# One fp32 transformer block on one core: the selected-key attention placed right behind the top-k search in program order

## The chip, the core and the metric

The kernel runs on one core of a Trainium2 chip. The core's engines are TensorE (PE, matmuls; PEld is its weight load), VectorE (DVE), ScalarE (ACT), GpSimd (POOL) and SyncE (SP, which here only issues DMAs; ACT issues some too). Each engine runs its own instructions in their order, and waits for the others through semaphores. The metric is the device time of one execution in microseconds (us), lower is better; the times given are the median of several runs.

## What is computed

One transformer block on 512 rows of width 1024, in fp32: a mixer of three attention branches whose outputs are projected up, gated and added, then attention to a memory of 256 rows, then a SwiGLU. Cut to the mixer, which the change touches, and to the part behind it:

```python
p = _split_columns(u @ w_in)
o_a = _stick_breaking(...)                 # first branch
o_b = _dsa_attention(..., q_idx, k_idx, w_idx)   # second branch, on selected keys
o_c = _nsa_attention(...)                  # third branch
g = sigmoid(p['g_merge'].reshape(B, S, 3, D_MODEL))
merged = g[:, :, 0] * (o_a @ w_up[0]) + g[:, :, 1] * (o_b @ w_up[1]) + g[:, :, 2] * (o_c @ w_up[2])
h = x + merged @ w_out
kv = (_rmsnorm(mem, g_kv) @ w_kv)          # memory keys and values: no input from the mixer
```

In the second branch an index score of each row against each earlier row is made, the 128 largest of them are found (`top_k`), and the softmax runs over these keys alone.

## The kernel before

Rows are held in NT = 4 tiles of 128, columns in NK = 8 tiles of 128. An fp32 matmul is made of three passes of a reduced fp32 type, high·high, high·low and low·high (mm3, L91 to L96; the rows of the profile name them L94, L95, L96 in the order in which the scheduler put them; one of them is called a step below). So every weight block is loaded by SP (L80), cast to its high part by ACT (L58) and subtracted to its low part (L66), by DVE for `load_split` (three buffers) and by POOL for `load_fill` (two buffers).

The program is written stage by stage, and a scheduler gives each engine its order when the kernel is built: what stands earlier in the text has priority, and later work is drawn forward where the scheduler's own estimate sees an engine free. On the chip the order is then fixed. Moving a stage in the text therefore changes with what its instructions are interleaved. The stages that matter, in the order of the text before:

- The third branch's attention, per row tile three `rows_attention` or `cmp_attention` calls (L570 to L610) into one accumulator `av` (one PSUM bank). A call makes per head a score (L292, L293) into a bank of `gm` (two banks), DVE adds the mask and reduces it (L578), ACT takes the exponential (L579); the rows are scaled (L588 on DVE for the selected keys, L586 on ACT else), transposed by PE (L565) into `ps` (three banks), copied to SBUF (L60 by DVE for the selected keys, L58 by ACT else) and multiplied with the values (L101, two matmuls of two passes: x4 in the rows).
- Gates of the first branch, `fill_gate(0, f)` for f from 3 on: 24 steps into a bank of `gf` (two banks), then a tanh (L373). Then `merge_up(0, "a")` (merge a below): per f 6 steps `gf<-o_hi..` and a DVE product L388, 48 steps in all.
- Gates of the third branch, `fill_gate(2, f)`, 8 of 24 steps of 512 columns.
- The top-k search: 16 rounds over three tiles of score rows, each round a MAX8 (L615) and a MATCH_REPLACE8 (L616), all on DVE.
- `merge_up(2, "c")` (merge c): 48 steps into `gm`, 8 L388 on DVE, 8 additions on POOL (L404).
- L638 turns the searched score rows into a mask (three DVE instructions on SBUF), and the selected-key attention follows, 16 heads in four row tiles (scores `gm<-kb_hi,qi`, value products `av<-pt,vb`).
- Gates of the second branch for half of the rows, `fill_gate(1, f, S // 2)`: 8 of 24 steps of 256 columns.
- The memory's keys and values (L660 to L683): its rows `h` are loaded on ACT's queue (L664), normed (a square on ACT, L127; ten or so DVE instructions of one column, L115 to L120; a scaling, L129), transposed (L133) and multiplied with weights (48 steps of 512 columns, L94 to L96 on `mg_hi`, `mg_lo`). Then comes the merge of the second branch.

In the order that the chip runs before, merge a goes along with the third branch's last row tile while DVE searches; the third branch's gates and merge c follow, and then the selected-key attention, with the second branch's gates between its instructions on PE.

Of the kernel before, what the change touches and what calls it, by code (L numbers as in the profile page):

```python
# [18 lines left out]
NK = D // P  # L19
# [7 lines left out]
def block_kernel(ctx: ExitStack, tc: tile.TileContext, A, out, dbg=None):  # L27
# [6 lines left out]
    def dump(name, ap):  # L34
        if dbg and name in dbg:
            nc.sync.dma_start(dbg[name], ap)
# [25 lines left out]
    def split(dst_hi, dst_lo, src, hi_eng=None, lo_eng=None, scale=None):  # L62

        if scale is None:
            copy(hi_eng or nc.scalar, dst_hi, src)
            (lo_eng or nc.vector).tensor_sub(dst_lo, src, dst_hi.bitcast(F32))  # L66
        else:
            nc.scalar.activation(dst_hi, src, AF.Copy, scale=scale)
            nc.vector.scalar_tensor_tensor(dst_lo, src, scale, dst_hi.bitcast(F32), op0=ALU.mult, op1=ALU.subtract)

    def ring(pl, bufs, hi_eng=None, lo_eng=None):

        def load(shape, parts, lo_eng=lo_eng):
            n = shape[0] * shape[1]
            raw = pl.tile([P, WT], F32, name="raw", bufs=bufs[0])
            rv = raw[:, :n].rearrange("p (k n) -> p k n", n=shape[1])
            off = 0
            for src in parts:
                w = src.shape[-1]
                nc.sync.dma_start(rv[:, :, off:off + w], src)  # L80
                off += w
            hi = pl.tile([P, WT], F32R, name="whi", bufs=bufs[1])
            lo = pl.tile([P, WT], F32R, name="wlo", bufs=bufs[1])
            split(hi[:, :n], lo[:, :n], raw[:, :n], hi_eng, lo_eng)
            return [t[:, :n].rearrange("p (k n) -> p k n", n=shape[1]) for t in (hi, lo)]
        return load

    load_split = ring(stage, (3, 3))
    load_fill = ring(fill, (2, 2), lo_eng=nc.gpsimd)
# [56 lines left out]
    def cc(c):  # L146
        return slice(c * P, (c + 1) * P)
# [4 lines left out]
    gf_ps = pm.enter_context(tc.tile_pool(name="gf_ps", bufs=2, space=PSUM))  # L152
# [3 lines left out]
    gm_ps = gf_ps  # L156
# [206 lines left out]
    early_g = 3  # L363

    def merge_gate(j, f, g, load, bank, cols=slice(0, S)):

        w = load((NK, P), [col_view(w_in, 2128 + j * D + f * P, P)])
        for k in range(NK):
            mm3(bank, [t[:, k, :] for t in w], [t[:, k, cols] for t in uT], k == 0, k == NK - 1)
        if j == 0 and f < early_g:  # L370
            nc.scalar.copy(g, bank)
        else:
            nc.scalar.activation(g, bank, AF.Tanh, scale=0.5)  # L373

    def fill_gate(j, f, n=S):
        g_t[j, f] = gp_.tile([P, S], F32, name="g", bufs=16)
        gp = gf_ps.tile([P, 512], F32, name="gf")
        merge_gate(j, f, g_t[j, f][:, :n], load_split if j == 1 and f % 2 else load_fill, gp[:, :n], slice(0, n))

    def load_up(j, fh, load):  # L380
        return load((2, 512), [A["w_up"][0, j].rearrange("(k p) n -> p k n", p=P)[:, :, fh * 512:(fh + 1) * 512]])

    def add_up(w, f, name, g, up, cols):

        fc = slice(f % 4 * P, f % 4 * P + P)
        for k in range(2):
            mm3(up, [t[:, k, fc] for t in w], [t[:, k, cols] for t in oT[name]], k == 0, k == 1)
        nc.vector.scalar_tensor_tensor(g, g, 1.0, up, op0=ALU.add, op1=ALU.mult)  # L388

    def merge_up(j, name, load, up_ps, n=S):  # L390
        for f in range(NK):
            if f % 4 == 0:
                w = load_up(j, f // 4, load)
            g, first = g_t[j, f][:, :n], g_t[0, f][:, :n]
            if j == 0 and f < early_g:
                with tc.issue_after(last_exp[0]):
                    nc.scalar.activation(g, g, AF.Tanh, scale=0.5)
            up = up_ps.tile([P, 512], F32, name=up_tag[up_ps is gf_ps])
            add_up(w, f, name, g, up[:, :n], slice(0, n))
            if j == 1:  # L400
                nc.vector.tensor_add(first, first, g)
                split(mg[0][:, f, :n], mg[1][:, f, :n], first, lo_eng=nc.gpsimd)
            elif j == 2:
                nc.gpsimd.tensor_add(first, first, g)  # L404
# [8 lines left out]
    gm_ps = pm.enter_context(tc.tile_pool(name="gm_ps", bufs=2, space=PSUM))  # L413
# [198 lines left out]
    def topk_rounds(i, n):  # L612
        for _ in range(n):
            m8 = mq.tile([P, 8], F32, name="m8", bufs=3)
            nc.vector.max(m8, score[i])  # L615
            nc.vector.match_replace(score[i], m8, score[i], -3e38)  # L616
# [6 lines left out]
        rows_attention(i, qc, kwin, vs["vwin"], causal_bias(i), gates[:, i, 2::3], o_ps, False, True)  # L623
        split(o_c[0][:, :, cc(i)], o_c[1][:, :, cc(i)], o_ps, scale=0.5)
    dump("o_c", o_c[0].bitcast(F32))
    for f in range(early_g, NK):
        fill_gate(0, f)
    merge_up(0, "a", load_fill, gf_ps)
    for f in range(NK):
        fill_gate(2, f)  # L630
    for r in range(16):
        for x in range(1, NT):
            topk_rounds(x, 1)
    merge_up(2, "c", load_split, gm_ps)


    for i in range(1, NT):
# [2 lines left out]
    for i in range(NT):  # L640
        o_ps = av_ps.tile([P, 2, P], F32, name="av")
        rows_attention(i, qb, kb, vs["vb"], score[i] if i else causal_bias(0), None, o_ps, True, True, nc.vector)
        split(o_b[0][:, :, cc(i)], o_b[1][:, :, cc(i)], o_ps, scale=0.5)
    dump("o_b", o_b[0].bitcast(F32))
    for f in range(NK):
        fill_gate(1, f, S // 2)
    mq_st.close()
# [278 lines left out]
```

## Time and profile before

| what | us |
|---|---|
| median of 3 runs (901.30 to 902.61) | 902.41 |
| the profiled execution | 901.59 |
| its span in the trace | 899.8 |
| PE busy within the span | 859.8 (96%) |
| DVE busy | 509.5 (57%) |
| ACT busy | 412.3 (46%) |
| POOL busy | 139.0 (15%) |

All times below are counted from the start of the span. The profiled execution lies 0.82 us below the median and 1.79 us above its own span. The page gives the shares, windows cut the span into stretches, the timeline has single instructions with the idle time ahead of each in square brackets and what ended it. Matmuls are pipelined, so a row's duration is longer than its distance to the next row: what a step costs is that distance.

### The profile page before, as it was taken

Reading aid. Unit: us, or ns where it says so; the run is one execution under the profiler, and the core shown is the slowest. Engines: PE = TensorE matmul, PEld = TensorE weight load, DVE = VectorE, ACT = ScalarE, POOL = GpSimd, SP = SyncE. Lnnn points to the kernel's source line nnn. Section 1 sums busy time; section 2 is a strip of 40 time slices with the busy share of each in tenths; the row PEclk is TensorE's granted clock in tenths of the full one; section 3 lists DMA queues with packets and bytes.
Section 4 is the critical chain, followed back from the end, with each engine's and each line's share of the span. In section 5 each row is a group of like instructions: output and inputs, shape, how many; then the busy total and the mean of one; then the engine's idle time right before and its main releaser. Section 6 shows DMA issues by size and latency. Waiting matters only on the chain.

```text
span 899.8 us, 13079 instructions
## 1 busy us (share of the span) xinstructions
PE 859.8 (96%) x5012; PEld 734.3 (82%) x5012; DVE 509.5 (57%) x1155; ACT 412.3 (46%) x779; POOL 139.0 (15%) x116
## 2 busy tenths in 40 slices
PE   5999999899999999899989999999999999999995
PEld 5987899887768877778878979998888888888884
DVE  4456378799992067676677758544434333322226
ACT  6488545567772234554655546432232233211123
POOL 4021232202224462230232020000000000000002
PEclk9999999999999999999999999999999999999998
DMA  9340114511212332558445514553333333332312
GB/s 322 84 110 24 52 49 121 139 48 34 62 48 71 94 94 71 186 173 241 128 148 187 178 48 131 179 160 93 94 95 101 105 98 94 117 94 93 97 45 93
DMA packets 93710, 99.00 MB, mean 110 GB/s; under 512 B 4656, under 2 KB 81616, under 8 KB 93648
## 3 DMA queue, kind: packets, MB, share of 16 engines
q1 hardware_dynamic: 91568, 92.75, 34.1%
q10 hardware_dynamic: 2080, 5.42, 1.8%
q8 instruction: 39, 0.64, 0.3%
q14 instruction: 23, 0.19, 0.1%
HBM read 96.06 MB, written 2.10 MB: 109 GB/s over the span
## 4 chain that ended last, share of the span: by engine, by line
PE 83%; DVE 8%; ACT 3%; DMA 3%; issue 2%; POOL 1%; SPq 0%; ACTq 0%; DVEq 0%; POOLq 0%
PE wo L95 9%; PE wo L96 9%; PE wo L94 9%; PE gf L94 5%; PE gf L96 5%; PE gf L95 5%; PE ff L96 4%; PE ff L94 4%; PE ff L95 4%; PE gm L94 3%; PE gm L95 3%; PE gm L96 3%; PE av L101 2%; PE y L96 2%; PE y L95 2%; PE y L94 2%
## 5 line engine op out<-in xcount | busy, mean ns | idle before, releaser
L58 ACT CAST whi<-raw 128x1024 fp32r<-128x1024 f32 (+1 forms) x167 | 174.9, 1050 | 289.0 <-PE y L96 78.9
L66 DVE TENSOR_TENSOR wlo<-raw,whi 128x1024 fp32r<-128x1024 f32 (+1 forms) x131 | 164.2, 1256 | 206.6 <-ACT whi L58 206.2
L66 POOL TENSOR_TENSOR wlo<-raw,whi 128x1024 fp32r<-128x1024 f32 x36 | 87.2, 2428 | 324.2 <-ACT whi L58 277.2
L95 PE MATMUL wo<-ut_lo,whi 128*128 128x256 f32 (+1 forms) x320 | 105.9, 331 | 0.0
L96 PE MATMUL wo<-ut_hi,wlo 128*128 128x256 f32 (+1 forms) x320 | 105.0, 328 | 0.0
L94 PE MATMUL wo<-ut_hi,whi 128*128 128x256 f32 (+1 forms) x320 | 104.7, 327 | 0.0
L96 PE MATMUL gf<-ut_hi,wlo 128*128 128x512 f32 (+1 forms) x192 | 70.0, 365 | 0.0
L94 PE MATMUL gf<-ut_hi,whi 128*128 128x512 f32 (+1 forms) x192 | 69.8, 364 | 0.0
L95 PE MATMUL gf<-ut_lo,whi 128*128 128x512 f32 (+1 forms) x192 | 69.5, 362 | 0.0
L94 PE MATMUL ff<-ut_hi,whi 128*128 128x512 f32 (+1 forms) x192 | 67.9, 354 | 0.0
L95 PE MATMUL ff<-ut_lo,whi 128*128 128x512 f32 (+1 forms) x192 | 67.9, 354 | 0.0
L96 PE MATMUL ff<-ut_hi,wlo 128*128 128x512 f32 (+1 forms) x192 | 67.9, 354 | 0.0
L95 PEld LDWEIGHTS wo<-ut_lo,whi 128*128 128x128 f32 x320 | 61.4, 192 | 6.3 <-issue 1.0
L94 PEld LDWEIGHTS wo<-ut_hi,whi 128*128 128x128 f32 x320 | 61.2, 191 | 5.7 <-issue 0.7
L96 PEld LDWEIGHTS wo<-ut_hi,wlo 128*128 128x128 f32 x320 | 61.3, 192 | 5.5 <-issue 0.4
L875 POOL TENSOR_TENSOR ut_hi<-ut_hi,ut_lo 128x512 f32<-128x512 f32 x4 | 5.0, 1274 | 367.0 <-ACT ut_hi L874 367.0
L94 PE MATMUL gm<-whi,ut_hi 128*128 128x256 f32 (+1 forms) x160 | 47.6, 298 | 0.0
L95 PE MATMUL gm<-wlo,ut_hi 128*128 128x256 f32 (+1 forms) x160 | 46.7, 292 | 0.0
L96 PE MATMUL gm<-whi,ut_lo 128*128 128x256 f32 (+1 forms) x160 | 46.6, 291 | 0.0
L96 PEld LDWEIGHTS gf<-ut_hi,wlo 128*128 128x128 f32 x192 | 36.2, 189 | 6.6 <-issue 1.9
L94 PEld LDWEIGHTS gf<-ut_hi,whi 128*128 128x128 f32 x192 | 36.2, 189 | 6.3 <-issue 1.5
L95 PEld LDWEIGHTS gf<-ut_lo,whi 128*128 128x128 f32 x192 | 36.3, 189 | 5.5 <-issue 0.8
(329 smaller groups left out, 2034.8 us busy)
## 6 DMA issues: line engine op xcount, KB each, us to landing
raw<-in_w_ffn_in_dram SPq DMA_DIRECT2D x56, 512.0 KB, 3.6
raw<-in_w_in_dram SPq DMA_DIRECT2D x46, 512.0 KB, 3.9
raw<-in_w_ffn_out_dram SPq DMA_DIRECT2D x22, 512.0 KB, 3.6
raw<-in_w_out_dram SPq DMA_DIRECT2D x16, 512.0 KB, 3.6
raw<-in_w_up_dram SPq DMA_DIRECT2D x8, 512.0 KB, 3.8
xt<-in_x_dram SPq DMA_DIRECT2D x4, 512.0 KB, 9.2
raw<-in_w_mem_kv_dram SPq DMA_DIRECT2D x4, 512.0 KB, 3.7
raw<-in_w_mem_q_dram SPq DMA_DIRECT2D x4, 512.0 KB, 3.7
```

Source lines behind the costliest of these rows:

```text
L58: nc.scalar.copy(dst, src)
L66: (lo_eng or nc.vector).tensor_sub(dst_lo, src, dst_hi.bitcast(F32))
L94: nc.tensor.matmul(dst, lh, rh, start=first, stop=False, skip_group_check=True)
L95: nc.tensor.matmul(dst, lh, rl, start=False, stop=False, skip_group_check=True)
L96: return nc.tensor.matmul(dst, ll, rh, start=False, stop=last, skip_group_check=True).ins
L101: nc.tensor.matmul(dst[64 * x:64 * x + 64], lhs[x], rhs[x], start=first, stop=last, skip_group_check=True)
L875: nc.gpsimd.tensor_mul(yo[:, n], yo[:, n], gain[:, n])
```

## The change

Five statements move: the first branch's late gates, merge a, the third branch's gates and merge c stand behind the selected-key attention instead of ahead of it, and the search follows directly on the third branch's attention. Nothing is added or taken away; every engine has the same instructions as before, in another order.

```diff
@@ -623,15 +623,9 @@
         rows_attention(i, qc, kwin, vs["vwin"], causal_bias(i), gates[:, i, 2::3], o_ps, False, True)
         split(o_c[0][:, :, cc(i)], o_c[1][:, :, cc(i)], o_ps, scale=0.5)
     dump("o_c", o_c[0].bitcast(F32))
-    for f in range(early_g, NK):
-        fill_gate(0, f)
-    merge_up(0, "a", load_fill, gf_ps)
-    for f in range(NK):
-        fill_gate(2, f)
     for r in range(16):
         for x in range(1, NT):
             topk_rounds(x, 1)
-    merge_up(2, "c", load_split, gm_ps)
 
 
     for i in range(1, NT):
@@ -642,6 +636,12 @@
         rows_attention(i, qb, kb, vs["vb"], score[i] if i else causal_bias(0), None, o_ps, True, True, nc.vector)
         split(o_b[0][:, :, cc(i)], o_b[1][:, :, cc(i)], o_ps, scale=0.5)
     dump("o_b", o_b[0].bitcast(F32))
+    for f in range(early_g, NK):
+        fill_gate(0, f)
+    merge_up(0, "a", load_fill, gf_ps)
+    for f in range(NK):
+        fill_gate(2, f)
+    merge_up(2, "c", load_split, gm_ps)
     for f in range(NK):
         fill_gate(1, f, S // 2)
     mq_st.close()
```

Three places of the order that this makes. The first is PE at the end of the third branch's attention (`vwin` its last values, `o_hi`, `o_lo` the first branch's output in merge a, `kb` the keys of the second branch). Before:

```order
L96 MATMUL gf<-o_hi,wlo 128x512
L94 MATMUL gf<-o_hi,whi 128x512
L101 MATMUL av<-pt,vwin 64x256 x2
L565 MATMUL ps<-cst,pr 128x128
L101 MATMUL av<-pt,vwin 64x256 x4
L565 MATMUL ps<-cst,pr 128x128 x3
L95 MATMUL gf<-o_lo,whi 128x512
L96 MATMUL gf<-o_hi,wlo 128x512
L94 MATMUL gf<-o_hi,whi 128x512
L95 MATMUL gf<-o_lo,whi 128x512
L101 MATMUL av<-pt,vwin 64x256 x2
```

After:

```order
L565 MATMUL ps<-cst,pr 128x128 x6
L101 MATMUL av<-pt,vwin 64x256 x2
L565 MATMUL ps<-cst,pr 128x128
L101 MATMUL av<-pt,vwin 64x256 x4
L565 MATMUL ps<-cst,pr 128x128 x3
L101 MATMUL av<-pt,vwin 64x256 x2
L292 MATMUL gm<-kb_hi,qi 128x128
L293 MATMUL gm<-kb_lo,qi 128x128
L292 MATMUL gm<-kb_hi,qi 128x128
L293 MATMUL gm<-kb_lo,qi 128x128
L94 MATMUL gf<-o_hi,whi 128x512
L95 MATMUL gf<-o_lo,whi 128x512
```

Behind the last value products `av<-pt,vwin` now stand the scores of the selected keys, and the steps of merge a that stood between the last transposes and value products have gone behind them.

The second is DVE at the end of the search (score_1246 to score_1248 are the three tiles of score rows; L638 before is L632 after; `gf` and `gm` are merge a's and merge c's banks). Before:

```order
L388 SCALAR_TENSOR_TENSOR g<-g,gf 128x512
L615 MAX m_3833<-score_1248 128x8
L388 SCALAR_TENSOR_TENSOR g<-g,gf 128x512
L616 MATCH_REPLACE score_1248<-m_3833,score_1248 128x512
L388 SCALAR_TENSOR_TENSOR g<-g,gf 128x512
L638 TENSOR_SCALAR score_1246<-score_1246 128x256
L638 TENSOR_SCALAR score_1247<-score_1247 128x384
L638 TENSOR_SCALAR score_1248<-score_1248 128x512
L388 SCALAR_TENSOR_TENSOR g<-g,gm 128x512 x4
L66 TENSOR_TENSOR wlo<-raw,whi 128x1024
L388 SCALAR_TENSOR_TENSOR g<-g,gm 128x512 x4
L578 ISA pr,nm<-gm,cst 128x128
```

After:

```order
L616 MATCH_REPLACE score_1248<-m_3325,score_1248 128x512
L632 TENSOR_SCALAR score_1246<-score_1246 128x256
L632 TENSOR_SCALAR score_1247<-score_1247 128x384
L69 SCALAR_TENSOR_TENSOR o_lo<-av,o_hi 128x2x128
L632 TENSOR_SCALAR score_1248<-score_1248 128x512
L578 ISA pr,nm<-gm,cst 128x128
L578 ISA nm 128x1
L578 ISA pr,nm<-gm,cst 128x128
L578 ISA nm 128x1
L388 SCALAR_TENSOR_TENSOR g<-g,gf 128x512
L578 ISA pr,nm<-gm,cst 128x128
```

The products L388 of merge a stood between the last rounds of the search, and those of merge c between the mask and the first reduction L578; now rounds, masks and reductions follow on each other, with one L69 (the low part of the third branch's output) among the masks.

The third is ACT, ahead of the norm of the memory's rows. Before:

```order
L68 ACTIVATE o_hi<-av 128x2x128
L58 CAST whi<-raw 128x1024
L373 ACTIVATE g<-gf 128x256
L68 ACTIVATE o_hi<-av 128x2x128
L664 DMA h_4412<-in_mem_dram 128x1024
L373 ACTIVATE g<-gf 128x256
L664 DMA h_4413<-in_mem_dram 128x1024
L140 DMA gain<-in_norm_mem_kv_dram 128x1024
L373 ACTIVATE g<-gf 128x256
L127 ACTIVATE h_4414,ss<-h_4412 128x1024
L127 ACTIVATE h_4415,ss<-h_4413 128x1024
```

After, first where the loads are issued, then where the norm stands:

```order
L68 ACTIVATE o_hi<-av 128x2x128 x4
L664 DMA h_4412<-in_mem_dram 128x1024
L664 DMA h_4413<-in_mem_dram 128x1024
L373 ACTIVATE g<-gf 128x512
L58 CAST whi<-raw 128x1024 x2
L373 ACTIVATE g<-gf 128x512
```

```order
L58 CAST whi<-raw 128x1024 x2
L140 DMA gain<-in_norm_mem_kv_dram 128x1024
L127 ACTIVATE h_4414,ss<-h_4412 128x1024
L373 ACTIVATE g<-gf 128x256
L58 CAST whi<-raw 128x1024
L127 ACTIVATE h_4415,ss<-h_4413 128x1024
L58 CAST whi<-raw 128x1024
L373 ACTIVATE g<-gf 128x256
```

The two loads L664 of the memory's rows were issued behind most of the second branch's tanhs (the forms 128x256); now they stand ahead of the third branch's tanhs (128x512), with eight of these between them and the first square L127.

## Rows read from the trace of the kernel before

**Rows 1.** The page: busy time by engine, and the chain that ended last.
```profile
PE 859.8 (96%) x5012; PEld 734.3 (82%) x5012; DVE 509.5 (57%) x1155; ACT 412.3 (46%) x779; POOL 139.0 (15%) x116
...
PE 83%; DVE 8%; ACT 3%; DMA 3%; issue 2%; POOL 1%; SPq 0%; ACTq 0%; DVEq 0%; POOLq 0%
```

**Rows 2.** Windows: us, busy (count) of PE, PEld, DVE, ACT, POOL; PE clock, DMA share, GB/s.
```profile
330.00:335.00 5.00, 4.63 (x35) 4.18 (x35) 4.51 (x21) 3.46 (x15) 2.58 (x2) 1.00 0.32 108
335.00:340.00 5.00, 3.75 (x27) 3.01 (x27) 4.86 (x13) 3.40 (x9) 2.46 (x1) 1.00 0.00 0
...
370.00:375.00 5.00, 2.72 (x24) 2.48 (x22) 4.96 (x3) 3.63 (x6) 4.52 (x2) 1.00 0.75 231
```

**Rows 3.** Groups of PE, 251.55 to 268.7: count, busy us, mean ns, idle before.
```profile
L565 PE MATMUL ps<-cst,pr 128*128 128x128 f32 x32 | 5.3, 279 | 0.0
...
L101 PE MATMUL av<-pt,vwin 128*64 128x256 f32 x16 | 2.4, 398 | 0.0
```

**Rows 4.** Timeline of PE: start, us, what, count [idle before, released by].
```profile
256.89 1.52 PE L101 MATMUL av<-pt,vsel 128*64 128x256 f32 x12
258.34 0.66 PE L565 MATMUL ps<-cst,pr 128*128 128x128 f32 x4
...
267.40 0.39 PE L94 MATMUL gf<-o_hi,whi 128*128 128x512 f32 x1
267.63 0.40 PE L95 MATMUL gf<-o_lo,whi 128*128 128x512 f32 x1
267.96 0.65 PE L101 MATMUL av<-pt,vwin 128*64 128x256 f32 x4
...
268.88 0.40 PE L94 MATMUL gf<-o_hi,whi 128*128 128x512 f32 x1
```

**Rows 5.** Groups of DVE, 251.93 to 272.5: one of them, with the idle time ahead.
```profile
L388 DVE SCALAR_TENSOR_TENSOR g<-g,gf 128x512 f32<-128x512 f32 x7 | 4.8, 685 | 0.5 <-PE gf L96 0.5
```

**Rows 6.** Timeline of DVE: the end of the search.
```profile
272.50 0.69 DVE L388 SCALAR_TENSOR_TENSOR g<-g,gf 128x512 f32<-128x512 f32 x1
273.11 3.09 DVE L638 TENSOR_SCALAR score<-score 128x256 f32<-128x256 f32 x3
```

**Rows 7.** Line 638 alone: shortest, median, longest in ns, forms.
```profile
L638 DVE TENSOR_SCALAR score<-score x3: 286/355/2621, 273.1 to 273.6; 128x256 f32<-128x256 f32 x1, 128x384 f32<-128x384 f32 x1, 128x512 f32<-128x512 f32 x1
```

**Rows 8.** Timeline of PE in the selected-key attention.
```profile
331.71 0.33 PE L292 MATMUL gm<-kb_hi,qi 128*128 128x128 f32 x1 [0.36 <-DVE nm L578]
...
339.93 0.44 PE L565 MATMUL ps<-cst,pr 128*128 128x128 f32 x2 [1.25 <-DVE pr L588]
```

**Rows 9.** Timeline of DVE at the same place.
```profile
337.85 2.29 DVE L588 TENSOR_SCALAR pr<-pr,sc 128x256 f32<-128x256 f32 x2
```

**Rows 10.** Timeline of PE, the memory's keys and values.
```profile
371.69 1.04 PE L133 MATMUL ps<-cst,h 128*128 128x128 f32 x8
...
376.99 1.09 PE L133 MATMUL ps<-cst,h 128*128 128x128 f32 x4 [4.27 <-DVE h L129]
...
378.31 0.63 PE L95 MATMUL gm<-wlo,mg_hi 128*128 128x512 f32 x1
...
390.31 0.39 PE L96 MATMUL gm<-whi,mg_lo 128*128 128x512 f32 x1
```

**Rows 11.** Timeline of DVE at the same place.
```profile
369.41 0.22 DVE L119 SCALAR_TENSOR_TENSOR rs<-rs 128x1 f32<-128x1 f32 x1
...
370.67 2.36 DVE L120 SCALAR_TENSOR_TENSOR rs<-rs 128x1 f32<-128x1 f32 x1
```

**Rows 12.** Timeline of ACT's queue: a load of the memory's rows.
```profile
359.24 0.33 ACTq L664 DMA_DIRECT2D h<-in_mem_dram  x1
```

**Rows 13.** Clock: windows of PE, with the granted clock behind the busy time.
```profile
172.50:173.00 0.50, 0.50 (x4) 0.50 0.00 0
...
378.00:379.00 1.00, 1.00 (x4) 0.50 0.00 0
```

**Rows 14.** Timeline of PE, the idle piece ahead of the first of these windows.
```profile
169.92 0.66 PE L253 MATMUL ps<-cst,stk 128*128 128x128 f32 x4 [1.46 <-DVE stk L66]
```

## The prediction, made before the changed kernel ran

> **What bounds the kernel now.** I read the page's busy shares and its chain first: PE is busy for 96% of the span and makes 83% of the chain that ended last; DVE, next on the chain, has 8% [rows 1]. So the kernel is a line of matmuls with few holes, and a change of order can only do three things: fill holes that PE has, open new ones, or change what a given run of matmuls costs. I then went through the stretch that moves, 250 to 391 us, in windows of 5 us, looking for PE below 5.00. Third-branch gates and most of merge c are full. Holes are in the selected-key attention, 0.37 us between 330 and 335 and 1.25 between 335 and 340 [rows 2], and in the stage of the memory's keys and values, where one piece of 4.27 us ends with DVE's scaling L129 [rows 10]. These holes are what the change can win, about 5.9 us. Then I laid the new order of each engine over the times of these rows, instruction by instruction, and looked where one engine would wait for another.
>
> **Part 1, the end of the search meets PE: +4.2 us.** PE's order differs from 251.55 on. Ahead of the selected keys' third score stand, in the new order, 12 steps of merge a, four short score matmuls, 32 transposes and 9 groups of value products (four of them `vwin`, as now in the same stretch) [rows 3]; the steps I counted in the order. A step costs 0.23 us (start to start) [rows 4]; a transpose 0.10 (eight in 1.04 against four in 0.66) [rows 4, 10]. A group of value products costs 0.43 when it follows another (three in 1.52 against 0.65 for one), and 0.34 more when it stands alone: from 267.63 to 268.88 lie two steps and one lone group, 1.25 - 0.46 = 0.79 [rows 4]. So PE has 12 x 0.23 = 2.8, 32 x 0.105 = 3.4, 9 x 0.43 = 3.9, 7 interruptions x 0.34 = 2.4 and 0.4 for the short scores, together 12.9 us of work.
> DVE needs longer. The search ends at 272.50 now, where the next row is a product L388 [rows 6]. Ahead of it in the same stretch lie seven other L388 of 0.60 each (start to start) with 0.5 us of waits, and an L69 with 0.39 of wait and 0.34 of its own [rows 5] (the L69 stands in the order too). Without them the search ends at 272.50 - 4.2 - 0.5 - 0.7 = 267.1 or so. The first two masks take 0.29 and 0.36, as the two undisturbed ones do now, and the third, the longest row, some 0.42 by the same step [rows 7], with an L69 of 0.34 among them, each about 0.06 less from start to start; so the first reduction is reached near 268.3 and ends at 268.6, and the third score, which needs its bank, starts near 268.7. From 251.55 that is 17.15 us against 12.9 of work: 4.2 us of new holes on PE, in pieces of about 0.6, 1.1, 0.85 and 2.05. Ends: 3.4 if lone groups and transposes cost PE more than counted, 5.0 if L69 waits for ACT as it does now.
>
> **Part 2, the selected keys' scores without gates between them: +2.4 us.** Before, the second branch's gates filled PE while a score waited for a bank; 90 steps of them stand in the attention. After, what is left of merge a fills, and the first of the third branch's gates. Sixteen scores need one of two banks, each free only when the reduction two ahead of it has ended. Where this wait shows now it is 0.36 [rows 8]. Ends: 0, if merge a's steps fill it as the gates did, and 16 x 0.36 = 5.8, if each score waits so. I take 2.4, from laying the orders side by side: pieces of 0.45, 1.1 and 0.8 where copies L60 and reductions alternate on DVE.
>
> **Part 3, the clock: +0.9 us.** A piece of 1.46 us of idle [rows 14] was followed by a granted clock of 0.50, the lower level of 1.2 GHz [rows 13], and the 4.27 us in the memory stage as well [rows 10, 13]. The piece of 1.25 was not: its window has 1.00 [rows 2]. The 2.05 us of part 1 lie above both short ones, with other pieces ahead of them. In the memory stage the lower level cost about 2.0 (worked out in part 5). I take less than half of that, since steps of DVE-bound attention stand in this stretch and wait anyhow; ends 0 and 3.
>
> **Part 4, what goes away in the attention: -1.6 and -1.7 us.** The holes of 0.37 and 1.25 [rows 2] belong to the order that is gone. The longer of them is one wait for L588 [rows 8]; on DVE two scalings took 2.29 there, while POOL ran its one instruction of 2.46 us [rows 9, 2]. In the new order POOL has no weight block at that place. Second, interruptions: the lone groups of value products fall from 16 to 11, since in the new order they stand in rows of eight and twelve: 5 x 0.34 = 1.7. Ends: 1 to 2.5 for it.
>
> **Part 5, the memory's keys and values: -4.9 us.** The stage lasts from 371.69 to 390.54 now, 18.85 us [rows 10]. Its work is 16 transposes, 1.7 us, and 48 steps at 0.23, 11.0 us. So 6.1 are lost: the hole of 4.27, and about 2.0 around it, most of it at the lower clock (at 378 to 379 a step's row lasts 0.63 instead of 0.40, with 0.50 granted) [rows 10, 13, 4]. The hole comes from the norm of the second row tile: two of its one-column instructions lasted 2.36 and about as much, where the same instruction takes 0.22 [rows 11], in a window in which POOL is busy for 4.52 of 5 us [rows 2]. The loads of these rows are issued at 359.24 [rows 12]; in the new order they are issued behind the attention's last outputs, some 60 us ahead of the stage, and the norms stand on ACT and DVE among the second branch's gates, which PE runs back to back. So transposes start at once. What stays: weights of the third block can be cast only when the last gate has freed its buffer, and ACT has the casts of the transposed rows in the same place: 1.0 us of idle. The stage then takes 1.7 + 11.0 + 1.0 = 13.7 to 13.9, and the gain is 4.9. Ends: 0.5 (below) and 6.1.
> Nothing else moves in time. The third branch's gates run as one row of matmuls before and after; their weights come two or three blocks ahead. POOL's additions L404 stand behind their old place but ahead of the second branch's blocks; I find a block late by 0.3 at most. Behind the stage the order is the same.
>
> **Sum.** 4.2 + 2.4 + 0.9 - 1.6 - 1.7 - 4.9 = -0.7 against the profiled 901.59 (span 899.8 and 1.79 outside), so 900.9. The profiled execution lies 0.82 below the median of the three runs, so the median should be **901.7**. What a measurement of this kernel can tell from no change is about 0.2%, 1.8 us: from 900.6 to 904.2 counts as the same.
>
> **A rule against it.** [rows 11] and [rows 9] show short DVE instructions that last over 2 us (0.22 for its like in rows 11) while POOL subtracts a weight block. The Trainium skill, "SBUF — State Buffer", section "SBUF: two separate sides", says the port pair that VectorE and GpSimd share is an exclusive lock, held for a whole instruction, and the other one blocks fully; both rows agree with it (2.36 us, and 2.29 us beside a POOL instruction of 2.46). By it the gain of part 5 holds only while no POOL block lies on the norms or on the low part of the stage's first weights.
>
> **Rivals.** (a) The new holes are short: 3.4 in part 1, 1.2 in part 2 and no lower clock. For it speaks that 36 of merge a's 48 steps are still there to fill the attention; against it, that PE's order is fixed and they stand where they stand. Sum -0.7 - 0.8 - 1.2 - 0.9 = -3.6, 898.8. (b) Slower: DVE bounds the selected-key attention. Every one of the 16 scores waits 0.36 for the reduction two ahead, with no gate between, so part 2 is 5.8 and the sum +2.7: 905.1. It decides from 4.9 us of such waits on, 0.31 a score. For it: DVE is busy for 4.86 of 5 us in the attention already [rows 2]. Against it: a part of that was the 2.29 us row, and products L388 are all that is added. (c) The norm is caught again: POOL subtracts its last blocks for the gates and two more at the end of the gates, as now; if these fall on the norm or the first weights of the stage, two instructions lose about 2.1 each, and part 5 gives 0.5 instead of 4.9. Sum +3.7: 906.1. Against it: the norms stand some ten us ahead of the gates' end.
>
> **How the numbers follow.** The forecast 0.43, (a) 0.36, (b) 0.14, (c) 0.07. Faster is (a) with 0.36, the same is the forecast with 0.43, slower is (b) and (c) with 0.21. The forecast's own range is 900.6 to 904.2. The whole range takes in most of (a), of which a tenth lies below 898.2, and (b) up to 905.2; left out are the rest of (b), (c) and the lower part of (a).
>
> **What would show it.** Right: PE windows between 252 and 269 with 3 to 5 us missing, a score head in the attention with a wait for L578 or L60, a clock below 1.00 at about 269 to 272, and the memory stage without a piece of idle over 1 us. Wrong: part 1, if the first selected-key reduction lies before 267; part 2, if the waits of `gm<-kb` sum to under 1 or over 5; part 5, if PE still waits for L129 there; the whole, if PE's gates of the third branch show idle time for weights.

## The result, and the profile after

The changed kernel takes 898.22 us in the median (6 runs), the kernel before 902.32 (6 runs): a ratio of 0.995, with a 95% interval of 0.9937 to 0.9963. It is faster by 4.1 us, where 901.7 and "the same" were forecast; a second comparison gave a smaller gain, 0.9976 (below). The profiled execution took 898.28 us, 3.3 less than that of before.

The page of the changed kernel, the same two parts as [rows 1]:

```profile
PE 856.3 (96%) x5012; PEld 731.7 (82%) x5012; DVE 507.8 (57%) x1155; ACT 411.5 (46%) x779; POOL 140.7 (16%) x116
...
PE 85%; DVE 7%; ACT 4%; issue 2%; DMA 1%; POOL 0%; ACTq 0%; DVEq 0%; POOLq 0%
```

PE's share is the same, and so is its idle time (40.0 us before, 40.2 after): holes went at some places and came at others. PE's busy time is 3.5 us less; rows at the lower clock count as busy for longer, and so do value products that stand alone. How the 3.5 divide between the two was not measured. The time went in several places. First the windows of 5 us, two of the kernel before, then those from 255 to 285 after (columns as in [rows 2]):

```profile
265.00:270.00 5.00, 5.00 (x30) 3.01 (x27) 4.61 (x15) 1.50 (x4) 1.53 (x1) 1.00 0.43 114
...
275.00:280.00 5.00, 5.00 (x23) 4.01 (x22) 1.20 (x1) 1.55 (x2) 1.87 (x2) 1.00 0.40 105
```

```profile
255.00:260.00 5.00, 4.59 (x30) 2.35 (x28) 5.00 (x19) 4.61 (x11) 0.00 (x0) 1.00 0.00 0
260.00:265.00 5.00, 4.09 (x30) 2.57 (x28) 5.00 (x16) 4.36 (x8) 2.00 (x1) 1.00 0.01 2
265.00:270.00 5.00, 2.79 (x16) 1.80 (x13) 4.73 (x18) 2.08 (x7) 0.36 (x1) 0.86 0.39 105
270.00:275.00 5.00, 5.00 (x26) 4.40 (x25) 4.24 (x18) 2.89 (x12) 0.00 (x0) 0.80 0.00 0
275.00:280.00 5.00, 3.94 (x23) 2.71 (x22) 4.38 (x16) 3.28 (x8) 1.67 (x1) 1.00 0.01 3
280.00:285.00 5.00, 4.79 (x26) 3.29 (x25) 4.79 (x16) 3.51 (x10) 0.70 (x1) 1.00 0.39 105
```

PE's busy time is 0.41, 0.91 and 2.21 short of 5.00 up to 270, 3.5 us of new holes, and 1.06 and 0.21 behind, 1.3; before, all of 255 to 325 was full. The clock is at 0.86 and 0.80 from 265 to 275. The PE rows at the end of these holes:

```profile
256.36 0.65 PE L101 MATMUL av<-pt,vsel 128*64 128x256 f32 x4 [0.40 <-ACT pt L58]
...
263.44 0.65 PE L101 MATMUL av<-pt,vwin 128*64 128x256 f32 x4 [0.87 <-ACT pt L58]
...
266.58 0.65 PE L101 MATMUL av<-pt,vwin 128*64 128x256 f32 x4 [0.73 <-ACT pt L58]
268.71 0.48 PE L292 MATMUL gm<-kb_hi,qi 128*128 128x128 f32 x1 [1.48 <-DVE nm L578]
...
279.71 0.50 PE L292 MATMUL gm<-kb_hi,qi 128*128 128x512 f32 x1 [1.06 <-DVE nm L578]
```

Two kinds: value products that wait for ACT's copy of the transposed rows (L58), and scores that wait for a reduction (L578). The longest, 1.48, is the third score of the selected keys, which starts at 268.71. On DVE, the search has ended at 267.00, where the masks begin, and the first reduction starts at 268.37:

```profile
267.00 0.55 DVE L632 TENSOR_SCALAR score<-score 128x256 f32<-128x256 f32 x2
...
268.37 0.28 DVE L578 CUSTOM_DVE_ANT_0 pr<-gm,cst 128x128 f32<-128x128 f32 x1
```

Then the stage of the memory's keys and values, against [rows 10]:

```profile
374.73 1.47 PE L133 MATMUL ps<-cst,h 128*128 128x128 f32 x12
376.67 0.50 PE L94 MATMUL gm<-whi,mg_hi 128*128 128x512 f32 x1 [0.47 <-ACT mg_hi L58]
...
388.45 0.39 PE L96 MATMUL gm<-whi,mg_lo 128*128 128x512 f32 x1
```

It starts 2.7 us later than before, counted from the same transposes near 251 in both traces (123.5 us behind them instead of 120.8), has no hole but 0.47 and 0.25 for ACT's casts, and ends at 388.84, where the next row stands: 14.1 us instead of 19.0. On ACT's queue the loads are issued at 300.84, and DVE ends the norms at 367.3:

```profile
300.84 1.69 ACTq L664 DMA_DIRECT2D h<-in_mem_dram  x2
```

```profile
356.89 2.34 DVE L119 SCALAR_TENSOR_TENSOR rs<-rs 128x1 f32<-128x1 f32 x1
...
362.75 2.37 DVE L120 SCALAR_TENSOR_TENSOR rs<-rs 128x1 f32<-128x1 f32 x1
...
366.05 1.28 DVE L129 SCALAR_TENSOR_TENSOR h<-h,rs,gain 128x1024 f32<-128x1024 f32 x1
```

Instructions of one column still take 2.3 us here as in [rows 11], but PE has gates to run until 374.73. So far the balance is +2.7 and -4.9. Another 1.5 us is won near 467 us, in a stage that the change doesn't touch: the granted clock fell there in the trace of before and not in this one. The rest, +0.4, lies ahead of 251.

### The profile page after: what moved, and what is told of

Read it like the earlier page. It is cut to its first block, busy times and chain, and to the rows that moved or that the text cites. A ratio compares the mean times of both kernels' runs of the same rounds, so it can differ in the third digit from the quotient of the medians.

```text
span 896.5 us, 13084 instructions
## 1 busy us (share of the span) xinstructions
PE 856.3 (96%) x5012; PEld 731.7 (82%) x5012; DVE 507.8 (57%) x1155; ACT 411.5 (46%) x779; POOL 140.7 (16%) x116
## 4 chain that ended last, share of the span: by engine, by line
PE 85%; DVE 7%; ACT 4%; issue 2%; DMA 1%; POOL 0%; ACTq 0%; DVEq 0%; POOLq 0%
PE wo L95 9%; PE wo L96 9%; PE wo L94 9%; PE gf L94 6%; PE gf L95 6%; PE gf L96 6%; PE ff L94 4%; PE ff L95 4%; PE ff L96 4%; PE gm L94 3%; PE gm L95 3%; PE gm L96 3%; PE y L96 2%; PE y L94 2%; PE y L95 2%; PE av L101 2%
## 5 line engine op out<-in xcount | busy, mean ns | idle before, releaser
L58 ACT CAST whi<-raw 128x1024 fp32r<-128x1024 f32 (+1 forms) x167 | 174.8, 1048 | 292.4 <-PE y L96 78.9
L66 POOL TENSOR_TENSOR wlo<-raw,whi 128x1024 fp32r<-128x1024 f32 x36 | 88.9, 2474 | 312.9 <-ACT whi L58 267.1
```

The lines of the kernel that those rows point to most:

```text
L58: nc.scalar.copy(dst, src)
```

## The experiments

Each was compared with the kernel before on the same chip in the same session.

**The loads of the memory's rows put back.** To the changed kernel (`tanh_of[j, f]` holds the tanh of gate f of branch j + 1):

```diff
...
-    for c in range(2):
-        nc.scalar.dma_start(h[c], A["mem"][0, cc(c), :])
-    gain = load_gain(kvp, "norm_mem_kv")
+    with tc.issue_after(tanh_of[1, 2]):
+        nc.scalar.dma_start(h[0], A["mem"][0, cc(0), :])
+    with tc.issue_after(tanh_of[1, 3]):
+        nc.scalar.dma_start(h[1], A["mem"][0, cc(1), :])
+        gain = load_gain(kvp, "norm_mem_kv")
```

Expected: 

> The changed kernel, with one thing put back: the two loads of the memory's rows (and of the gain) are issued only behind the tanhs of the second branch's third and fourth gate, as in the kernel before, so that the norms again end at the stage of the memory's keys and values. Theory 1 (the gain is the memory stage: 19.0 us before, 14.1 after): the hole of about 4 us ahead of the transposes and the lower clock behind it come back, 898.2 + 4.9 = 903. Rival theory 2 (the gain lies in the attention and the gates that now run back to back): the loads do not matter, 898 to 899.

Measured: 905.16 us against 901.15 of before, ratio 1.0042 (1.0027 to 1.0058), and 6.0 more than the changed kernel in the same session. PE's row at the hole, then DVE's:

```profile
379.41 1.09 PE L133 MATMUL ps<-cst,h 128*128 128x128 f32 x4 [5.35 <-DVE h L129]
```

```profile
371.60 2.36 DVE L120 SCALAR_TENSOR_TENSOR rs<-rs 128x1 f32<-128x1 f32 x1
...
375.02 2.29 DVE L119 SCALAR_TENSOR_TENSOR rs<-rs 128x1 f32<-128x1 f32 x1
```

The one-column instructions stand beside POOL's two subtractions:

```profile
371.35 5.94 POOL L66 TENSOR_TENSOR wlo<-raw,whi 128x1024 fp32r<-128x1024 f32 x2 [8.95 <-ACT whi L58]
```

The hole is back, longer than before (5.35: the second load is issued at 361.86, 1.3 later than before, and the first scaling also waited 0.65 for the gain), and the stage takes 20.5 us. Near 473 the lower clock of before is back, too. So the loss is 6.0 where 4.9 was expected. In this order the early loads are the gain of the memory stage; without them the change is a loss.

**Merge a and its gates left ahead of the search.** Against the changed kernel, only this stands elsewhere:

```diff
+    for f in range(early_g, NK):
+        fill_gate(0, f)
+    merge_up(0, "a", load_fill, gf_ps)
     for r in range(16):
...
-    for f in range(early_g, NK):
-        fill_gate(0, f)
-    merge_up(0, "a", load_fill, gf_ps)
     for f in range(NK):
         fill_gate(2, f)
     merge_up(2, "c", load_split, gm_ps)
```

Expected: 

> The changed kernel, with the first branch's late gates and merge a left ahead of the search: only the third branch's gates and merge c stand behind the selected-key attention. Theory 1: merge a fills PE while DVE searches, so that the 3.5 us of holes between 251 and 269 and the lower clock behind them (1 to 1.7) go, at the price of some 1.7 for lone value-product groups and 0.6 a product on DVE; the memory stage stays at 14. 895 to 897. Rival: the holes belong to the search itself, which DVE ends no earlier, and only move behind merge a: 898 to 899.

Measured: 891.57, ratio 0.9894 (0.988 to 0.9909). It beats both kernels by far, and lies 3.4 us below the expected range. The windows 250 to 300 of this one, then of the changed kernel:

```profile
250.00:300.00 50.00, 50.00 (x286) 34.04 (x285) 43.17 (x132) 28.67 (x68) 9.85 (x4) 1.00 0.16 44
```

```profile
250.00:300.00 50.00, 45.19 (x258) 31.57 (x256) 43.01 (x134) 27.43 (x67) 7.12 (x3) 0.97 0.12 32
```

With merge a, PE is full for 50 us; without it, 45.19. All 4.8 us of new holes went, of which the expectation had counted 3.5. The memory stage starts 3.2 us earlier than before (117.6 us behind the transposes near 251) and takes 14.1. The selected-key attention has no hole either, since the third branch's gates stand in it.

**Merge c alone moved.** The kernel before with `merge_up(2, "c", ...)` behind the attention, ahead of the second branch's gates.

Expected: 

> The kernel before, with merge c alone moved behind the selected-key attention; all gates and merge a stay where they were. Theory 1: the attention ends 11 us ahead of the second branch's gates' old place, the memory's rows are normed under the gates, and the memory stage falls from 19.0 to 14: 902.3 - 4.9 = 897.4, with the attention's old holes of 1.6 left or filled by merge c (896 to 898). Theory 2: the gates and merge a are not moved, so next to nothing is won: 901.5 to 902.5.

Measured: 892.43, ratio 0.9904 (0.9888 to 0.9921). That is a gain of 8.7 us where 4.9 was expected, and one moved statement gives more than twice the gain of all of them. The memory stage takes 14.1 us and starts 2.9 earlier than before (117.9 us behind the transposes near 251): the old holes of [rows 8] are gone (PE waits for no reduction and no scaling up to the stage), and so is a third one, of 0.65, which stood in merge c before:

```profile
325.00:330.00 5.00, 4.35 (x22) 3.30 (x21) 3.18 (x7) 1.05 (x1) 5.00 (x4) 1.00 0.30 105
```

Together these are 2.3 of the 2.9; the expectation had left the first two open and had not counted the third. With the 4.9 of the stage the 2.9 are 7.8 of the gain of 8.7; the rest was not followed to its place.

**The third branch's gates put back ahead of the search**, merge a left behind:

```diff
+    for f in range(NK):
+        fill_gate(2, f)
     for r in range(16):
...
     merge_up(0, "a", load_fill, gf_ps)
-    for f in range(NK):
-        fill_gate(2, f)
     merge_up(2, "c", load_split, gm_ps)
```

Expected: 

> The changed kernel, with the third branch's gates put back ahead of the search; the first branch's late gates, merge a and merge c stay behind the selected-key attention. If the holes between 251 and 269 come from PE having nothing to do while DVE searches, any 45 us of gates fill them as well as merge a does: no hole over 0.5 there, memory stage 14, 890 to 894. If it is merge a's leaving the search that costs (its products on DVE then stand in the attention, its steps are missing there), the loss stays: 896 to 899.

Measured: 890.78, ratio 0.987 (0.9855 to 0.9885).

```profile
250.00:300.00 50.00, 49.65 (x267) 36.72 (x266) 34.50 (x117) 30.60 (x71) 12.24 (x5) 1.00 0.18 47
```

0.35 us of holes in these 50. So it isn't merge a that the search needs: the third branch's gates beside it do as well, and the changed kernel had taken both supplies away at once.

**The changed kernel and the kernel before, once more.** 

Expected: 

> The changed kernel once more, for a second trace of it. If the clock in the stage near 467 us, which the change does not touch, belongs to the change, it is at its upper level again here (as in the first trace, against 0.64 over 4 us in the kernel before); if it comes and goes by itself, it is lower in some of these traces and not in others. Time 898.2 either way within 1.5.

Expected: 

> The kernel before once more, for a second trace. The hole of 4.27 in the memory stage must be there again. If the lower clock near 469 us goes with the kernel before (as in its first trace and in the one with the late loads, and in none of the four others), it is there again; if it comes by chance after a hole of 2.3 us, it may be missing. Time 901 to 902.5.

Measured: 899.16 against 901.15, ratio 0.9976 (0.9966 to 0.9985), a gain of 2.0 us instead of 4.1; and 902.4 against 902.88 (1.0, 0.999 to 1.001). The second trace of before has the hole (4.44) and a memory stage of 20.5 us, but near 469 its clock stays up. One window of the first trace of before, and one of the second, at the same place behind a hole of 2.27 and 2.23 us (columns: PE busy, granted clock, DMA share, GB/s):

```profile
470.00:471.00 1.00, 1.00 (x7) 0.50 0.05 18
```

```profile
470.00:471.00 1.00, 1.00 (x11) 1.00 0.87 330
```

The hole is in every trace but the last two below, 2.2 to 2.3 us long, at 458 to 471 us by the order ahead of it, and the lower clock followed it in three traces (before, the late loads, and the late query weights below) and not in six. It doesn't belong to the change.

The holes near 269 behave likewise. Three traces have the same order and the same holes up to there, the changed kernel's two and that with late loads. Windows of 2 us from 269 in the changed kernel's first trace, in its second, and in that with late loads:

```profile
269.00:271.00 2.00, 2.00 (x8) 0.50 0.00 0
271.00:273.00 2.00, 2.00 (x11) 0.74 0.00 0
```

```profile
269.00:271.00 2.00, 2.00 (x9) 0.50 0.00 0
271.00:273.00 2.00, 2.00 (x8) 0.50 0.00 0
273.00:275.00 2.00, 2.00 (x10) 0.56 0.00 0
```

```profile
269.00:271.00 2.00, 2.00 (x12) 1.00 0.00 0
```

The clock fell for some 3 us, for 6, and not at all, and the memory stage started 123.5, 124.8 and 122.3 us behind the transposes near 251: up to 2.5 us for the clock alone.

**POOL's blocks moved away from the norm.** To the kernel before, an order on SyncE: the memory's query weights, whose low parts POOL subtracts, are fetched behind the last key and value weights (`last_dma[0]` is the transfer issued last).

```diff
...
+        kv_dma = last_dma[0]
...
+            with tc.issue_after(kv_dma):
-            w = load_fill((4, 256), ...
+                w = load_fill((4, 256), ...
```

Expected: 

> The kernel before, with one order added on SyncE: the first two blocks of the memory's query weights, whose low parts POOL subtracts, are fetched only behind the last block of the memory's key and value weights. DVE's order in the norm stays as it was. If POOL's two subtractions (4.84 us at 370.48) are what stretches the one-column instructions of the norm from 0.2 to 2.3 us, these go back to 0.2, the hole of 4.27 ahead of the transposes falls under 1, and with the lower clock behind it 4 to 6 us go: 895 to 897.5. If the hole comes from the late loads of the memory's rows or from ACT's squares, nothing of it changes: 901 to 902.5.

Measured: 898.18 against 902.88, ratio 0.9952 (0.9937 to 0.9967), from the place of two transfers in a queue. POOL's two subtractions in the kernel before:

```profile
370.48 4.84 POOL L66 TENSOR_TENSOR wlo<-raw,whi 128x1024 fp32r<-128x1024 f32 x2 [14.13 <-ACT whi L58]
```

With the edit, the norm's second half on DVE (L121, L122 and L131 are L119, L120 and L129 of before), POOL's next block, and PE's hole:

```profile
371.59 0.15 DVE L122 SCALAR_TENSOR_TENSOR rs<-rs 128x1 f32<-128x1 f32 x1
371.78 0.22 DVE L121 SCALAR_TENSOR_TENSOR rs<-rs 128x1 f32<-128x1 f32 x1
372.03 0.16 DVE L122 SCALAR_TENSOR_TENSOR rs<-rs 128x1 f32<-128x1 f32 x1
372.23 1.28 DVE L131 SCALAR_TENSOR_TENSOR h<-h,rs,gain 128x1024 f32<-128x1024 f32 x1
```

```profile
380.13 2.48 POOL L66 TENSOR_TENSOR wlo<-raw,whi 128x1024 fp32r<-128x1024 f32 x1 [23.84 <-ACT whi L58]
```

```profile
373.66 0.63 PE L135 MATMUL ps<-cst,h 128*128 128x128 f32 x4 [0.98 <-DVE h L131]
```

The same instructions that took 2.36 [rows 11] and 2.26 us take 0.15 and 0.22, the hole is 0.98 instead of 4.27 (the second row tile's norm began 0.9 later here, at 367.40), and the stage takes 14.5. The edit moves these blocks' casts on ACT away as well, so by itself it doesn't tell POOL from ACT; the next experiment moves a subtraction alone. The two together show that the long instructions of the norm, and with them the hole of before, come from POOL's subtractions.

**The same cause near 460 us.** In the order with merge a ahead of the search, the second query-weight block of the second half of the rows is subtracted by DVE instead of POOL (`lo_eng` set to `nc.vector` for it).

Expected: 

> The version with merge a left ahead of the search (891.6), and the second query-weight block of the second half on DVE instead of POOL. In all traces so far one one-column instruction of the norm near 460 to 468 us lasts 2.3 us beside POOL's subtraction, and PE has a hole of 2.25 there. If POOL's subtraction is the cause, the hole falls by about 1 us (DVE now spends 1.2 on the block itself, in the same place): 890.3 to 891. If not, the hole grows by 1.2: 892 to 893.

POOL and DVE in the version without this edit:

```profile
455.95 2.40 POOL L66 TENSOR_TENSOR wlo<-raw,whi 128x1024 fp32r<-128x1024 f32 x1 [0.90 <-POOL wlo L66]
```

```profile
456.05 2.31 DVE L120 SCALAR_TENSOR_TENSOR rs<-rs 128x1 f32<-128x1 f32 x1
```

The same instruction with the edit, then PE's transposes without and with it:

```profile
457.65 0.16 DVE L120 SCALAR_TENSOR_TENSOR rs<-rs 128x1 f32<-128x1 f32 x1
```

```profile
460.19 1.09 PE L133 MATMUL ps<-cst,u 128*128 128x128 f32 x8 [2.26 <-DVE rs L115]
```

```profile
459.64 1.09 PE L133 MATMUL ps<-cst,u 128*128 128x128 f32 x8
```

Measured: 890.28, ratio 0.9865 (0.9851 to 0.988) where the version without the edit had 0.9894; the spans of the two profiled executions are 888.4 and 889.6. The long instruction is short again, 0.16 instead of 2.31. The hole of 2.26 went to nothing (0.15 is left at the next transposes), but only half of that is the norm's: it is 1.1 us shorter, since DVE now does the block, and nine more steps of 0.12 stand ahead of the transposes in the new order. With the third branch's gates ahead of the search instead of merge a:

Expected: 

> The two best steps together: the third branch's gates ahead of the search and all else behind the selected-key attention (890.8), and the second query-weight block of the second half on DVE (1.3 won on the other order). If the two are independent, as their places 100 us apart suggest: 889.5, 888.8 to 890.3. If the place of the norm near 460 depends on the order ahead of it: 890.8.

Measured: 889.28 against 900.75 of before, ratio 0.9869 (0.9852 to 0.9885). That the two steps add up isn't shown: the span is 1.0 shorter (888.2 against 889.2), but by the ratio it stands with 0.987 and 0.9865 of the two above. Each of these three takes 11 to 13 us off the kernel before.

## Why the prediction was wrong

Its steps against the profiled execution, in us:

| step | forecast | measured | read from |
|---|---|---|---|
| part 1, holes up to 270 | +4.2 | +3.5 | windows 255 to 270 |
| part 2, holes behind | +2.4 | +1.3 | windows 275 to 285 |
| part 3, clock | +0.9 | +1.2 | start of the memory stage against the trace without a lower clock |
| part 4, attention | -3.3 | -3.3 | what is left over in that trace: start 1.5 later, with 4.8 of holes |
| part 5, memory stage | -4.9 | -4.9 | 19.0 to 14.1 |
| behind the stage | 0 | -1.5 | clock near 467 |
| ahead of 251 | 0 | +0.4 | start of the same transposes |
| sum | -0.7 | -3.3 | 901.59 to 898.28 |

**Part 1 was right in its mechanism and its place.** The search was forecast to end at 267.1 and ends at 267.00; the third score was forecast near 268.7 and starts at 268.71. The term was 0.7 too large, half of it for each of two reasons: PE reached this stretch at 251.93 instead of 251.55, the 0.4 from ahead of 251, and in the 16.8 us left it had 13.25 of work where 12.9 was counted. The pieces that the text names, 0.6, 1.1, 0.85 and 2.05, add up to 4.6 and not to its 4.2; they measured 0.40, 0.87, 0.73 and 1.48. The first three end with ACT's copies, which the text doesn't name.

**Part 2 was mis-sized**, 2.4 for 1.3. Scores do wait for reductions, once for 1.06 and once for 0.18, and do so in the trace without a lower clock as well; but of the three pieces taken (0.45, 1.1 and 0.8) only one came in its size. Merge a's steps stand between the scores at the other places. The value stood between 0 and 5.8 and rested on laying the orders side by side. These two terms are the step of the prediction that failed: it put 6.6 us of new holes where the runs showed 4.8, and with part 3 that turned a gain of 2.2 in the moved stretch into one of 0.7. The forecast is 2.6 off in all: this 1.5, another 1.5 for the clock near 467, which stood at nothing, and 0.4 the other way ahead of 251. Rival (a), with holes of 3.4 and 1.2, had both sizes; it had 0.36. That its 898.8 lies so near the measured 898.22 is luck in part, since it had no lower clock behind the holes, where 1.2 was measured, and nothing for the 1.5 either.

**Part 3** lay within its ends, 0 to 3: three traces of the same order show 0, 1.2 and 2.5. One value for it was more than the trace could give. The text then took the clock as a cost of new holes alone. That the kernel before loses to the clock at holes of its own, and by how much differs from one execution to the next (19.0 and 20.5 us for its memory stage, 1.5 or nothing near 469), stood in no term. The step "behind the stage the order is the same" was true of the order, and wrong of the time in these two executions. This may be why the gain is 4.1 in one comparison and 2.0 in another; that is not shown, since no execution of the kernel before in the second comparison has a trace.

**Part 5** came out as forecast: 14.1 us where 13.7 to 13.9 was forecast, with 0.7 of idle time for ACT's casts where 1.0 was. **Part 4** has the forecast sum, in part by luck. Its 3.3 is what the other rows leave over. The holes of 1.6 are gone as forecast; about 0.6 is from the hole in merge c (4.35 of 5 us busy between 325 and 330 before, 4.91 at the same steps after), which stood in no term. That leaves 1.1 for the interruptions, where 1.7 was forecast; they were not measured apart, but PE's value products `vb` take 5.3 us instead of 6.5 in the same 40 passes.

**Rival (c)** had the mechanism and not the time: POOL did stretch the norm's instructions (2.34 and 2.37), 7 us before anyone waited for them. **Rival (b)** didn't come: two waits of scores on reductions, not sixteen. The rule of the Trainium skill, "SBUF — State Buffer", section "SBUF: two separate sides", that the shared port pair is an exclusive lock, agrees with the traces: 0.15 without POOL's block, 2.36 beside it, and POOL's own subtraction took 3.38 beside a DVE subtraction in the changed kernel instead of 2.40. The 2.29 us of [rows 9] are two scalings, of which one lasted 2.03.

**What I did not see** is that the change was two changes. Work behind the attention gives the memory's loads and norms time, worth 4.9; the 11 us of merge c were enough for it. Work ahead of it keeps PE busy while DVE searches, and the change gave away all of it. The sum had both terms with opposite signs, and the experiments showed that they can be had separately.

## What to carry to other kernels

When a change moves several stages past an engine-bound one, price the supply of work left beside that stage and the head start given to the stage behind as two separate edits; here one of the moved statements gave 8.7 us by itself, and all of them together 2 to 4. A one-column instruction that lasts 2.3 us in a trace may not be slow but waiting: look at what POOL does in that moment. If PE waits behind it, moving POOL's block is worth a trial (4.7 us here); if PE has other work until then, as in the changed kernel, it costs nothing. A term for the clock behind a short hole should stand as a range on both sides, for the kernel before as well as after.

## What the runs showed of the hardware

The granted clock differed between traces behind the same hole. Behind the 2.2 to 2.3 us near 467 it fell to 0.50, the lower level of 1.2 GHz, in three of nine traces; behind the holes ahead of 269, of which the last is 1.48, in two of three. With it a difference of 1.2 to 2.5 us at one place comes and goes, which is as much as the smallest effect argued about here. What decides it was not found.

A DVE SCALAR_TENSOR_TENSOR on 128 x 1 elements lasted as long as the POOL subtraction of 128 x 1024 that it stood beside: 0.15 to 0.22 us became 2.36, 2.26 and 2.33 at three places of the kernel before (370, 373 and 464 us), each on the way of PE, and 2.34 and 2.37 at two places of the changed kernel, where nobody waited. The wait is inside the row's own duration: the views name DVE, and not POOL, as what PE waited for.
